# Softmax over rows of 512: the last block's VectorE multiply as seven per-row multiplies

## The chip, the core and the metric

The kernel runs on one core of one Trainium2 chip. The metric is the device time of one execution in microseconds (us), as the median of several executions.

## The reference

The input `x` has 16 x 1024 rows of 512 float32 values. Each row is divided by a temperature of 0.5 and put through a softmax:

```python
x_scaled = x / 0.5
x_max = np.max(x_scaled, axis=-1, keepdims=True)
exp_x = np.exp(x_scaled - x_max)
return (exp_x / np.sum(exp_x, axis=-1, keepdims=True)).astype(np.float32)
```

Every input byte is read once and every output byte is written once: 33.55 MB each way.

## The kernel before

The 16384 rows are cut into 8 chunks (`c` = 0 to 7) of 2048 rows. Each of the 128 partitions holds 16 rows of a chunk, 8192 floats, so a chunk is one SBUF tile `xt` of 4 MB. There are six such tiles; chunks 6 and 7 reuse the tiles of chunks 0 and 1. All work on a chunk is done in place in its tile.

A chunk is worked on in blocks, a block being a range of the 16 rows of a partition: chunk 0 has three blocks (4, 4 and 8 rows), chunks 1 to 6 have one of 16 rows, and chunk 7 has two of 8 rows, which makes 11 blocks (`n` = 11). A block goes through these steps:

- `shift(i)`: VectorE takes the negated row maxima (`negmax`, line 92) and doubles them (`bias`, line 96). If the chunk isn't loaded yet, its load is issued first on SyncE's queue (line 75).
- `exponentials(i, rows)`: ScalarE computes exp(2x + bias) row by row, and adds up each row on the way (`sums`, line 122).
- `scale_vector(i)`: VectorE takes the reciprocals of the sums (`recip`, line 143) and multiplies the first `k` rows of the block with them, all in one `tensor_mul` in which the reciprocals are broadcast along the 512 columns (line 145). `k` is 12 of 16 rows, 7 of 8, or 4 of 4.
- `scale_scalar(i)`: ScalarE multiplies the other rows, one by one, with a per-partition scale (line 156).
- `store(i)`: when the chunk's last block is done, ScalarE's queue issues one store of the whole chunk, 4 MB (line 166).

The order of instructions on each engine is written out by hand (`tc.manual_schedule()`): in each round the exponentials of block i + 1 come first, then the multiplies of block i, the maxima of block i + 2, and the store. Loads of chunks 1 and 3 are issued on ScalarE's queue, and two rows of chunk 7 come in by GpSimd (line 111), started in the middle of chunk 5. SyncE ends the program with a `nop` (line 192) that waits for everything named in the list `finished`, and the end of the program (shown as line 223) waits for what is left, the last store.

The change is in `scale_vector`, for the last block alone (`i == n - 1`): the second half of chunk 7, eight rows, of which VectorE multiplies seven and ScalarE one. Behind it in the program stands only the store of chunk 7.

Of the kernel before, what the change touches and what calls it, by code (L numbers as in the profile page):

```python
# [1 line left out]

# [4 lines left out]


@with_exitstack
def kernel(  # L10
    ctx: ExitStack,
    tc: tile.TileContext,
    x: bass.AP,
    out: bass.AP,
):
    nc = tc.nc
    fp32 = mybir.dt.float32
    P = nc.NUM_PARTITIONS
    AX = mybir.AxisListType.X
    EXP = mybir.ActivationFunctionType.Exp  # L20
    COPY = mybir.ActivationFunctionType.Copy
    MAX = mybir.AluOpType.max

    D = x.shape[-1]
    xf = x.flatten_outer_dims()
    of = out.flatten_outer_dims()
    N = xf.shape[0]

    G = 16
    C = N // (P * G)
    assert C * P * G == N
    xr = xf.rearrange("(c p g) d -> c p g d", p=P, g=G)
    outr = of.rearrange("(c p g) d -> c p g d", p=P, g=G)
    WHOLE = [(0, G)]
    LATE = 2
    LOADS = [[(0, 4), (4, G)]] + [WHOLE] * 6 + [[(0, G - LATE)]]
    BLOCKS = [[(0, 4), (4, 8), (8, G)]] + [WHOLE] * 6 + [[(0, 8), (8, G)]]  # L40
    STORES = [WHOLE] * 8
    BMAX = 16
    BUFS = 6

    data = ctx.enter_context(tc.tile_pool(name="data", bufs=BUFS))
    stats = ctx.enter_context(tc.tile_pool(name="stats", bufs=6))

    ctx.enter_context(tc.manual_schedule())


    warm = stats.tile([P, 1], fp32, name="warm", bufs=1)
    nc.vector.memset(warm, 0.0)  # L52
    nc.scalar.activation(out=warm, in_=warm, func=EXP)  # L53

    chunks = {}
    blocks = [(c, lo, hi) for c in range(C) for lo, hi in BLOCKS[c]]
    n = len(blocks)
    biases, sums, recips = {}, {}, {}

    finished = []  # L60
    data_wait = mybir.DependencyInfo(
        mybir.DependencyClass.Sync, mybir.DependencyReason.DATA
    )
    for c in range(BUFS):
        chunks[c] = data.tile([P, G, D], fp32, name="xt")

    loaded = set()

    def load(c, queue):
        loaded.add(c)  # L70
        if c >= BUFS:
            chunks[c] = chunks[c - BUFS]
        xt = chunks[c]
        for lo, hi in LOADS[c]:
            part = queue.dma_start(out=xt[:, lo:hi, :], in_=xr[c][:, lo:hi, :])  # L75
            if c == 1:
                tc.add_manual_dep(
                    part.ins, finished[0], data_wait, reason="first rows come alone"
                )
            finished.append(part.ins.name)  # L80

    load(0, nc.sync)
    for c in (1, 3):
        load(c, nc.scalar)

    def shift(i):
        c, lo, hi = blocks[i]
        if c not in loaded:
            load(c, nc.sync)
        b = hi - lo  # L90
        negmax = stats.tile([P, BMAX], fp32, name="negmax")
        nc.vector.tensor_reduce(  # L92
            negmax[:, 0:b], chunks[c][:, lo:hi, :], axis=AX, op=MAX, negate=True
        )
        biases[i] = stats.tile([P, BMAX], fp32, name="bias")
        nc.vector.tensor_scalar_mul(biases[i][:, 0:b], negmax[:, 0:b], 2.0)  # L96

    def load_last_rows(signal):
        seen = stats.tile([P, 1], fp32, name="seen", bufs=1)
        copied = nc.gpsimd.tensor_copy(out=seen, in_=signal)  # L105
        finished.append(copied.ins.name)
        c = C - 1
        to = chunks[c - BUFS][:, G - LATE : G, :]
        of_ = xr[c][:, G - LATE : G, :]
        for p0, p1 in ((P - 2, P), (0, P - 2)):  # L110
            part = nc.gpsimd.dma_start(  # L111
                out=to[p0:p1], in_=of_[p0:p1], max_dma_last_dim=4 * D
            )
            finished.append(part.ins.name)

    def exponentials(i, rows):
        c, lo, hi = blocks[i]
        if i not in sums:
            sums[i] = stats.tile([P, BMAX], fp32, name="sums")
        for g in rows:  # L120
            row = chunks[c][:, lo + g, :]
            nc.scalar.activation(  # L122
                out=row,
                in_=row,
                func=EXP,
                bias=biases[i][:, g : g + 1],
                scale=2.0,
                accum_out=sums[i][:, g : g + 1],
            )
            if c == BUFS - 1 and g == 10:  # L130
                load_last_rows(sums[i][:, g : g + 1])


    def scalar_rows(i):
        c, lo, hi = blocks[i]
        return 4 if hi - lo == G else (hi - lo) // 8

    def scale_vector(i):
        c, lo, hi = blocks[i]
        b = hi - lo  # L140
        k = b - scalar_rows(i)
        recips[i] = stats.tile([P, BMAX], fp32, name="recip")
        nc.vector.reciprocal(recips[i][:, 0:b], sums[i][:, 0:b])  # L143
        rows = chunks[c][:, lo : lo + k, :]
        last = nc.vector.tensor_mul(  # L145
            rows, rows, recips[i][:, 0:k].unsqueeze(2).broadcast_to((P, k, D))
        )
        if i == n - 1:
            finished.append(last.ins.name)

    def scale_scalar(i):
        c, lo, hi = blocks[i]
        b = hi - lo
        for g in range(b - scalar_rows(i), b):
            row = chunks[c][:, lo + g, :]
            last = nc.scalar.activation(  # L156
                out=row, in_=row, func=COPY, scale=recips[i][:, g : g + 1]
            )
            if i == n - 1:
                finished.append(last.ins.name)  # L160

    def store(i):
        c, _, end = blocks[i]
        for lo, hi in STORES[c]:
            if hi == end:
                part = nc.scalar.dma_start(
                    out=outr[c][:, lo:hi, :], in_=chunks[c][:, lo:hi, :]
                )
                if c < C - 1:
                    finished.append(part.ins.name)  # L170

    shift(0)
    shift(1)

    def rows(i):
        c, lo, hi = blocks[i]
        cut = 6 if c == 1 else hi - lo
        return range(cut), range(cut, hi - lo)

    exponentials(0, rows(0)[0])  # L180
    for i in range(n):
        if i + 1 < n:
            exponentials(i + 1, rows(i + 1)[0])
        scale_vector(i)
        scale_scalar(i)
        if i + 2 < n:
            shift(i + 2)
        store(i)
        if i + 1 < n:
            exponentials(i + 1, rows(i + 1)[1])  # L190

    seen = nc.sync.nop()
    info = mybir.DependencyInfo(
        mybir.DependencyClass.Sync, mybir.DependencyReason.DATA
    )
    for name in finished:
        tc.add_manual_dep(seen.ins, name, info, reason="leaves one wait for the end")


# [1 line left out]
_INS = ['x']  # L201
_OUTS = [((16, 1024, 512), 'float32')]


# [23 lines left out]
```

## Time and profile before

| What | Value |
|---|---|
| median of 3 runs | 161.92 us (161.68 to 162.12) |
| profiled execution | 161.71 us |
| its span in the profile | 159.9 us |
| VectorE (DVE) busy | 128.3 us, 80% |
| ScalarE (ACT) busy | 109.6 us, 69% |
| GpSimd (POOL) busy | 1.9 us, 1% |
| bytes moved by DMA | 67.13 MB, mean 420 GB/s over the span |

The profile is one execution; its span begins and ends within the 161.71 us of that execution, with 1.8 us outside it. DVE, ACT, POOL and SP are the engines; a name with a q behind it (ACTq) is the engine's queue, which issues DMAs and waits on semaphores. An operation's row gives line, engine, operation, output and input tile, shape in partitions x elements, count, busy time and mean duration.

### The profile page before, as it was taken

How to read it: one execution, taken by the hardware profiler on the slowest of the kernel's cores; microseconds unless marked ns; L12 is line 12 of the kernel's file. 1: busy time of each engine (PE TensorE's matmuls, PEld its weight loads, DVE VectorE, ACT ScalarE, POOL GpSimd, SP SyncE). 2: the span in 40 equal slices, each digit the busy share in tenths (PEclk: the TensorE clock that was granted, in tenths of full speed). 3: DMA queues.
4: the chain of work that ended last, by engine and by line, in shares of the span. 5: the costliest groups of instructions: out<-in, count | busy, mean ns of one | idle time of the engine just before them, and what ended most of it. 6: DMA issues, size and time to landing. Idle time of an engine off the chain costs nothing.

```text
span 159.9 us, 422 instructions
## 1 busy us (share of the span) xinstructions
DVE 128.3 (80%) x45; ACT 109.6 (69%) x285; POOL 1.9 (1%) x7
## 2 busy tenths in 40 slices
DVE  0600599999999999999999999999999999955000
ACT  3070072924899999599959995999699899980000
POOL 0000000000000000000000000040000000000000
DMA  5999999999999999999999989898999999999994
GB/s 189 467 459 459 393 393 508 410 393 467 451 320 461 402 402 508 402 393 484 434 393 443 467 380 492 370 483 384 415 454 436 416 516 393 393 475 443 393 443 205
DMA packets 2642, 67.13 MB, mean 420 GB/s; under 512 B 336, under 2 KB 336, under 8 KB 464
## 3 DMA queue, kind: packets, MB, share of 16 engines
q10 hardware_dynamic: 1440, 41.94, 60.8%
q1 hardware_dynamic: 1008, 24.64, 36.5%
q0 software_dynamic: 192, 0.52, 0.8%
q14 instruction: 2, 0.02, 0.0%
HBM read 33.55 MB, written 33.55 MB: 420 GB/s over the span
## 4 chain that ended last, share of the span: by engine, by line
DVE 66%; ACT 10%; DMA 10%; issue 4%; SPq 0%
DVE negmax L92 39%; DVE xt L145 25%; ACT xt L122 10%; DMA xt<-in_x_dram 10%; DVE recip L143 1%; DVE bias L96 1%; SPq L75 0%
## 5 line engine op out<-in xcount | busy, mean ns | idle before, releaser
L122 ACT ACTIVATE xt<-xt,bias 128x512 f32<-128x512 f32 x128 | 90.4, 708 | 32.9 <-DVE bias L96 31.6
L92 DVE TENSOR_REDUCE negmax<-xt 128x16 f32<-128x8192 f32 (+2 forms) x11 | 69.9, 6353 | 14.2 <-DMA xt<-in_x_dram 14.2
L145 DVE TENSOR_TENSOR xt<-xt,recip 128x6144 f32<-128x6144 f32 (+2 forms) x11 | 55.6, 5056 | 0.4
L122 ACT ACTIVATION_READ_ACCUMULATOR xt<-xt,bias 128x1 f32 x128 | 23.9, 187 | 0.0
L156 ACT ACTIVATE xt<-xt,recip 128x512 f32<-128x512 f32 x27 | 17.3, 706 | 0.0
L143 DVE RECIPROCAL recip<-sums 128x16 f32<-128x16 f32 (+2 forms) x11 | 2.4, 220 | 2.1 <-ACT xt L122 2.1
L96 DVE TENSOR_SCALAR bias<-negmax 128x16 f32<-128x16 f32 (+2 forms) x11 | 1.9, 173 | 0.4
L53 ACT ACT_TABLE_LOAD x1 | 1.3, 1283 | 0.7 <-PEq L212 0.7
L111 POOL DMA_DIRECT2D xt<-in_x_dram x2 | 1.5, 744 | 0.5 <-issue 0.5
L105 POOL COPY seen<-sums 128x1 f32<-128x1 f32 x1 | 0.2, 186 | 105.2 <-ACT xt L122 105.2
L52 DVE MEMSET warm<- 128x1 f32 x1 | 0.1, 59 | 0.8 <-PEq L212 0.8
L53 ACT ACTIVATE warm<-warm 128x1 f32<-128x1 f32 x1 | 0.2, 203 | 0.0
L212 POOL MEMSET const-bfloat16-1.0<- 128x1 bf16 x1 | 0.1, 96 | 0.0
L212 POOL MEMSET const-uint8-127<- 128x1 uint8 x1 | 0.1, 96 | 0.0
L212 POOL MEMSET const-float32-0.0<- 128x1 f32 x1 | 0.1, 93 | 0.2 <-issue 0.2
L212 POOL MEMSET const-float32-1.0<- 128x1 f32 x1 | 0.1, 93 | 0.0
## 6 DMA issues: line engine op xcount, KB each, us to landing
out_dram<-xt ACTq DMA_DIRECT2D x8, 4096.0 KB, 20.9
xt<-in_x_dram SPq DMA_DIRECT2D x4, 4096.0 KB, 45.3
xt<-in_x_dram ACTq DMA_DIRECT2D x2, 4096.0 KB, 31.4
xt<-in_x_dram SPq DMA_DIRECT2D x1, 3584.0 KB, 25.3
xt<-in_x_dram SPq DMA_DIRECT2D x1, 3072.0 KB, 16.4
xt<-in_x_dram SPq DMA_DIRECT2D x1, 1024.0 KB, 4.7
xt<-in_x_dram POOLq DMA_DIRECT2D x1, 504.0 KB, 19.2
xt<-in_x_dram POOLq DMA_DIRECT2D x1, 8.0 KB, 8.6
```

The costliest lines, as they stand in the source:

```text
L52: nc.vector.memset(warm, 0.0)
L53: nc.scalar.activation(out=warm, in_=warm, func=EXP)
L92: nc.vector.tensor_reduce(negmax[:, 0:b], chunks[c][:, lo:hi, :], axis=AX, op=MAX, negate=True)
L96: nc.vector.tensor_scalar_mul(biases[i][:, 0:b], negmax[:, 0:b], 2.0)
L105: copied = nc.gpsimd.tensor_copy(out=seen, in_=signal)
L111: part = nc.gpsimd.dma_start(out=to[p0:p1], in_=of_[p0:p1], max_dma_last_dim=4 * D)
L122: nc.scalar.activation(out=row, in_=row, func=EXP, bias=biases[i][:, g : g + 1], scale=2.0, accum_out=sums[i][:, g : g + 1],)
L143: nc.vector.reciprocal(recips[i][:, 0:b], sums[i][:, 0:b])
L145: last = nc.vector.tensor_mul(rows, rows, recips[i][:, 0:k].unsqueeze(2).broadcast_to((P, k, D)))
L156: last = nc.scalar.activation(out=row, in_=row, func=COPY, scale=recips[i][:, g : g + 1])
L212: nc = _bacc.Bacc("TRN2", target_bir_lowering=False, num_devices=1)
```

## The change

In the last block VectorE no longer multiplies seven rows by one `tensor_mul` with a broadcast operand, but each row of 512 columns by a `tensor_scalar_mul` whose scalar is one reciprocal per partition. The other ten blocks keep the one `tensor_mul`. The end of the program waits for the last of the seven.

```diff
@@ -141,12 +141,16 @@
         k = b - scalar_rows(i)
         recips[i] = stats.tile([P, BMAX], fp32, name="recip")
         nc.vector.reciprocal(recips[i][:, 0:b], sums[i][:, 0:b])
+        if i == n - 1:
+            for g in range(k):
+                row = chunks[c][:, lo + g, :]
+                last = nc.vector.tensor_scalar_mul(row, row, recips[i][:, g : g + 1])
+            finished.append(last.ins.name)
+            return
         rows = chunks[c][:, lo : lo + k, :]
-        last = nc.vector.tensor_mul(
+        nc.vector.tensor_mul(
             rows, rows, recips[i][:, 0:k].unsqueeze(2).broadcast_to((P, k, D))
         )
-        if i == n - 1:
-            finished.append(last.ins.name)
```

## Prediction

> **What bounds the kernel now.** I read the page first, its DMA lines before anything else, because a kernel that reads and writes every byte once can be held by its transfers whatever its engines do.
>
> ```profile
> DMA  5999999999999999999999989898999999999994
> ...
> HBM read 33.55 MB, written 33.55 MB: 420 GB/s over the span
> ```
>
> The DMA engines are busy in every slice between the first and the last, those in which VectorE and ScalarE have nothing left to do included. Next I read the chain of work that ended last, and the timeline of the end.
>
> ```profile
> 142.00 0.02 issue
> 142.02 0.21 DVE recip L143
> 142.24 0.02 issue
> 142.26 3.89 DVE xt L145
> ```
>
> ```profile
> 141.89 1.32 ACT L156 ACTIVATE xt<-xt,recip 128x512 f32<-128x512 f32 x2
> 142.02 0.20 DVE L143 RECIPROCAL recip<-sums 128x8 f32<-128x8 f32 x1 [1.89 <-ACT xt L122]
> 142.26 3.89 DVE L145 TENSOR_TENSOR xt<-xt,recip 128x3584 f32<-128x3584 f32 x1
> 146.24 0.34 ACTq L166 DMA_DIRECT2D out_dram<-xt  x1
> ```
>
> The chain stops with the instruction of the change: the last multiply runs from 142.26 to 146.15, and the last store is issued at 146.24, 0.09 us later. Taken alone this says that a shorter multiply ends the kernel earlier. But 13.7 us of span follow, which the chain doesn't explain. SyncE's waits say what they are, and the DMA issues of the last two stores, asked one by one (the store of chunk 6, issued at 135.85 in the timeline, then that of chunk 7), say how long each took from issue to landing:
>
> ```profile
> SPq L223 <- DMA out_dram<-xt: 9.5, 1, 9.5
> ```
>
> ```profile
> out_dram<-xt ACTq DMA_DIRECT2D x1, 4096.0 KB, 13.6
> ```
>
> ```profile
> out_dram<-xt ACTq DMA_DIRECT2D x1, 4096.0 KB, 12.8
> ```
>
> So chunk 6 lands at 135.85 + 13.6 = 149.45, 3.2 us after the last store was issued, and chunk 7 at 146.24 + 12.8 = 159.04, and then the span is over but for 0.9 us. The landings are 9.6 us apart though the issues were 10.4 apart. What a store needs by itself is its bytes over the rate, so I read the windows (length, busy time of DVE, ACT and POOL, then the clock, the share of the 16 DMA engines, and GB/s):
>
> ```profile
> 142.30:146.20 3.90, 3.85 (x1) 0.91 (x2) 0.00 (x0) 1.00 1.03 445
> 146.60:156.30 9.70, 0.00 (x0) 0.00 (x0) 0.00 (x0) 1.00 1.00 432
> ...
> 146.60:147.80 1.20, 0.00 (x0) 0.00 (x0) 0.00 (x0) 1.00 1.01 437
> 147.80:149.00 1.20, 0.00 (x0) 0.00 (x0) 0.00 (x0) 1.00 1.02 437
> 149.00:150.20 1.20, 0.00 (x0) 0.00 (x0) 0.00 (x0) 1.00 1.01 437
> ```
>
> 4.194 MB at 432 GB/s take 9.7 us. That is the distance between the two landings. The engines were fully busy while the last multiply ran (1.03) and across the change from one store to the next (1.01, 1.02, 1.01; shares slightly over 1 come from counting a packet where it starts). The last store spends its first three microseconds standing behind the store before it. What bounds the end is DMA throughput and not the multiply, in spite of the chain.
>
> **The change part by part.** Durations are from the groups with shapes kept apart:
>
> ```profile
> L145 DVE TENSOR_TENSOR xt<-xt,recip 128x6144 f32<-128x6144 f32 x6 | 39.4, 6558 | 0.2
> L145 DVE TENSOR_TENSOR xt<-xt,recip 128x3584 f32<-128x3584 f32 x3 | 11.7, 3892 | 0.1
> ...
> L96 DVE TENSOR_SCALAR bias<-negmax 128x16 f32<-128x16 f32 x6 | 1.0, 175 | 0.2
> ...
> L96 DVE TENSOR_SCALAR bias<-negmax 128x4 f32<-128x4 f32 x2 | 0.3, 171 | 0.1
> ```
>
> *Removed:* one TENSOR_TENSOR of 3584 elements, 3.89 us, on the path to the issue of the last store.
>
> *Added:* seven TENSOR_SCALAR of 512 elements with one gap of 0.02 us (the chain's "issue" pieces) between each two. The trace has no TENSOR_SCALAR of that length and none with a per-partition scalar, so I bound it. Slow end, if it streams like the multiply: (6558 - 3892) / (6144 - 3584) = 1.04 ns an element and 3892 - 3584 x 1.04 = 160 ns fixed, so 693 ns a row and 7 x 0.693 + 6 x 0.02 = 4.97 us. Slower still, at ScalarE's price for the same row (706 ns, the 27 rows of L156) with a semaphore wait of 0.02 before each as well: 7 x 0.706 + 7 x 0.02 + 6 x 0.02 = 5.20 us. Fast end: the 171 ns of the four-element row, as if length cost nothing, 7 x 0.171 + 0.12 = 1.32 us. The TENSOR_SCALAR rows lie nearest in kind: twelve more elements cost 4 ns, 0.33 ns each, a third of the multiply's slope; that is thin, since it rests on 4 ns. I take 0.45, between them and nearer the row of the same operation: 171 + 508 x 0.45 = 400 ns, so 7 x 0.400 + 0.12 = 2.92 us. VectorE is done about 1.0 us sooner and the last store is issued at about 145.3, with 1.3 us later (147.5) and 2.6 us earlier (143.7) as the ends. ScalarE's own row ends by 143.21, so below that its row would be what is late.
>
> [...]
>
> *On the path or beside it:* neither matters for the end, unless the store comes too late for its turn. With the previous store's packets still running when it is issued, an earlier issue only stands longer in the queue: worth 0. For a later issue the slack is this. The windows show packets starting in rounds of 16, one every 1.21 us, so eight rounds make a store (9.7 / 1.21); in windows of 0.2 us the last store's eighth round starts between 157.0 and 157.4, so its first began 7 x 1.21 us before, near 148.6. From issue to first packet the trace shows one uncovered case, the first load: issued at 0.74, and the DMA share starts in the window 1.70 to 1.80, 1.0 us. So an issue as late as 147.5 to 147.6 still finds its turn, 1.3 us of cover. One engine of the 16 runs a round ahead (the share is 0.95 in the last round, 156.3 to 157.5); it would run dry earlier, but it also finishes a round before the others, so its idle time is free. The slowest bound, 5.20 us, is 1.31 us longer than now and just fits.
>
> *Moved:* nothing. No queue order changes; the store remains the only thing behind the waiting instruction on ACTq, and no maxima, load or exponential follows on VectorE. POOL's work ended long before. The reciprocals and ScalarE's row 15 are as before. `finished` names the last of seven instead of the one; SyncE passes that wait at 149.5 together with chunk 6's landing, so it costs nothing, and even 1.3 us later it would still be early.
>
> *The sum:* span 159.9 + 0 us, plus 1.8 outside it, is the profiled 161.7; that execution lies 0.2 us under the median of the runs. I forecast the median, 161.9.
>
> **The rivals.** *The seven rows cost more than the cover (slower).* Place: the issue of the last store. It decides from 3.89 + 1.3 = 5.2 us for the seven, 725 ns a row with its gap taken off; each microsecond beyond is a microsecond of the end. A row at what ScalarE needs for an exponential with its read-out of the sum (708 + 187 = 895 ns) would make 6.39 us, 2.5 later, less 1.3: about 163.1. To be seen as slower it needs over 5.7 us, 800 ns a row. For it: the trace doesn't show this operation. Against: every VectorE slope here is at most 1.04 ns an element with 160 to 175 ns fixed, for elementwise work. 8%.
>
> *The landing follows the issue (faster).* If the 12.8 us were a latency of the store and not a place in a queue, the end would come as much sooner as the multiply: 161.9 - 1.0 = 160.9, at the fast end of the bounds (2.6 us sooner) 159.3. For it: the chain ends in the multiply. Against: the 9.6 us between landings, and no idle share at the boundary. 10%.
>
> *The change doesn't do what it says.* The rows might run no faster than the old multiply, 4.97 us. Then the issue is at 147.3, still inside the cover: 161.9. This belongs to no change.
>
> **How the numbers follow.** About 0.3%, 0.49 us, is what a measurement of this kernel can tell from no change; the three runs lie 0.44 us apart. No change gets 0.82, faster 0.10, slower 0.08. The range: no change at 161.9 with half a microsecond for the scatter of medians, 161.4 to 162.4. All bounds of the unknown cost, from 1.32 to 5.20 us, give the same end, so they don't widen it, and both other cases, 18% together, stay outside.
>
> **What would show it.** Right: seven TENSOR_SCALAR of 128x512 in place of the last TENSOR_TENSOR, at about 0.4 us; the last store issued near 145.3; its time from issue to landing longer by what the issue is earlier (13.8 us in place of 12.8); the landing near 159.0 and the span at 159.9; the DMA share 1.0 across 148.6. The step on the row's price is wrong if the rows take 0.69 us; the end shouldn't notice. The forecast is wrong if issue to landing stays at 12.8 while the issue moves, or if a window between 147 and 149 shows DMA engines idle.

## The result and the profile after

The changed kernel takes 162.29 us (median of 22 runs) where the kernel before takes 162.04 (22 runs): ratio 1.0016, 95% interval 1.0009 to 1.0024. It is slower by a quarter of a microsecond. That is inside the predicted range and less than the 0.3% that I had called measurable, but it is a difference, and I had forecast none. The profiled execution took 162.25 us with a span of 160.3; 1.95 us lie outside the span, where the kernel before had 1.8.

The step that the change is about went nearly as forecast. First the timeline of the changed kernel at the end, and the group of the new operation:

```profile
142.05 0.20 DVE L143 RECIPROCAL recip<-sums 128x8 f32<-128x8 f32 x1 [1.89 <-ACT xt L122]
142.29 2.86 DVE L147 TENSOR_SCALAR xt<-xt,recip 128x512 f32<-128x512 f32 x7
145.24 0.34 ACTq L170 DMA_DIRECT2D out_dram<-xt  x1
```

```profile
L147 DVE TENSOR_SCALAR xt<-xt,recip 128x512 f32<-128x512 f32 x7 | 2.9, 480 | 0.0
```

Seven rows take 2.86 us where one multiply took 3.89, and the last store is issued at 145.24. A single row reads 480 ns, but 7 x 480 = 3.36 us is more than the 2.86 us they occupy: neighbouring rows overlap, and one row costs 0.41 us of the engine's time. Next the two last stores, asked one by one (chunk 6's, issued at 135.88, then chunk 7's), SyncE's wait for the last, and the windows across the boundary between the stores:

```profile
out_dram<-xt ACTq DMA_DIRECT2D x1, 4096.0 KB, 13.9
```

```profile
out_dram<-xt ACTq DMA_DIRECT2D x1, 4096.0 KB, 14.2
```

```profile
SPq L227 <- DMA out_dram<-xt: 9.5, 1, 9.5
```

```profile
146.60:147.80 1.20, 0.00 (x0) 0.00 (x0) 0.00 (x0) 1.00 1.01 437
147.80:149.00 1.20, 0.00 (x0) 0.00 (x0) 0.00 (x0) 1.00 1.02 437
149.00:150.20 1.20, 0.00 (x0) 0.00 (x0) 0.00 (x0) 1.00 1.01 437
```

The store goes out 1.0 us sooner and takes 1.4 us longer (14.2 against 12.8). The landings, 149.8 and 159.4, are again 9.6 us apart, SyncE again waits 9.5 us, and the DMA engines are as full as before. The microsecond that VectorE gained became waiting time in the DMA queue. Inside the span nothing came of it, and the 0.4 us by which this one span is longer is scatter: the spans of the kernel before, in the executions timed beside the experiments below, average 160.32, 160.27, 160.22 and 160.32 us over 35, 29, 35 and 29 executions, those of the changed kernel 160.30, 160.13 and 160.31 over 22, 12 and 12.

What stays is the time outside the span. Taken as time less span of each execution and averaged, it is 1.78, 1.77, 1.78 and 1.78 us in those runs of the kernel before, and 2.00, 1.97 and 2.00 in those of the changed kernel. One execution scatters by 0.03 us in the kernel before, which is no more than spans given to 0.1 us make by rounding, and by 0.10 to 0.12 in the changed kernel. The difference is 0.2 us, nearly all of the 0.25. In the profile only the DMA queue that it names "instruction" (q14) shows anything behind the span; a packet on it, 8 KB here (82 GB/s over the 0.1 us of the last window below), is called an instruction fetch below, after that name. Its line for the window from 155 to 165 us, kernel before and changed kernel (packets, MB, share of 16 engines):

```profile
q14 instruction: 1, 0.01, 0.3%
```

```profile
q14 instruction: 2, 0.02, 0.5%
```

The changed kernel has one packet more there, and the window 162.1 to 162.2 alone holds it, 1.8 to 1.9 us behind the end of the span (160.3):

```profile
q14 instruction: 1, 0.01, 20.2%
```

### The profile page after: what moved, and what is told of

The parts are those of the page before. It is cut to its first block, busy times and chain, and to the rows that moved or that the text cites. A ratio compares the mean times of both kernels' runs of the same rounds, so it can differ in the third digit from the quotient of the medians.

```text
span 160.3 us, 428 instructions
## 1 busy us (share of the span) xinstructions
DVE 127.3 (79%) x51; ACT 109.5 (68%) x285; POOL 1.9 (1%) x7
## 4 chain that ended last, share of the span: by engine, by line
DVE 65%; DMA 10%; ACT 10%; issue 4%; DVEq 0%; SPq 0%
DVE negmax L92 39%; DVE xt L151 23%; DMA xt<-in_x_dram 10%; ACT xt L122 10%; DVE xt L147 2%; DVE recip L143 1%; DVE bias L96 1%; DVEq L227 0%; SPq L75 0%
## 5 line engine op out<-in xcount | busy, mean ns | idle before, releaser
L92 DVE TENSOR_REDUCE negmax<-xt 128x16 f32<-128x8192 f32 (+2 forms) x11 | 69.9, 6352 | 14.2 <-DMA xt<-in_x_dram 14.2
L151 DVE TENSOR_TENSOR xt<-xt,recip 128x6144 f32<-128x6144 f32 (+2 forms) x10 | 51.7, 5171 | 0.3
L147 DVE TENSOR_SCALAR xt<-xt,recip 128x512 f32<-128x512 f32 x7 | 2.9, 480 | 0.0
```

Of the source, the lines that this page charges most:

```text
L92: nc.vector.tensor_reduce(negmax[:, 0:b], chunks[c][:, lo:hi, :], axis=AX, op=MAX, negate=True)
L147: last = nc.vector.tensor_scalar_mul(row, row, recips[i][:, g : g + 1])
L151: nc.vector.tensor_mul(rows, rows, recips[i][:, 0:k].unsqueeze(2).broadcast_to((P, k, D)))
```

## The experiments

**Is there a difference, and does it come with the issue of the store or with the instructions?** Two of these runs are the two kernels again, unchanged.

> The kernel before once more, unchanged, timed as if it were a new kernel. It measures what two equal programs can differ by. All theories expect a ratio of 1.000 with an interval that holds 1. If the 0.16% of the change is of the size that two loads of the same program differ by (theory 'scatter'), this ratio may lie as far from 1 as 0.1 to 0.2%.

Measured: 161.94 us (12 runs), ratio 0.9998 (0.9987 to 1.0008); 1.78 us outside the span. Equal programs are equal, to 0.1%.

> The changed kernel once more, beside the others on the same chip. If the loss belongs to the change, the ratio is again 1.0016, within about 0.001 (some 0.25 us). Theory 'scatter': the ratio is nearer to 1.000.

Measured: 162.07 us, ratio 0.9997 (0.9981 to 1.0012). The time alone doesn't repeat the loss here, since its spans average 160.13; twelve executions of a span that scatters by some tenths can't show 0.2 us. The time outside the span can: 1.97. The profiled execution of this run is one that doesn't have the loss (161.72 us with a span of 159.9, 1.8 outside), and in it the window 155 to 165 has a single instruction packet. So the extra packet and the loss were absent together in this one execution.

> The kernel before, but its last multiply covers four of the seven rows (three rows of each partition in the last block stay unscaled). As many instructions as before, of the same kinds; only the last store is issued earlier, by 3 x 512 x 1.04 ns = 1.6 us, at about 144.6. Theory 'issue' (an earlier issue of the last store lengthens the end): slower, by 0.2 to 0.4 us. Theory 'program' (six more VectorE instructions shift what the DMA engines do besides the stores, long before the end): the same as before, 1.000 within 0.001. Theory 'latency' (the landing follows the issue, the rival of the prediction): 1.6 us faster, ratio 0.990.

```diff
+        if i == n - 1:
+            k = 4
         rows = chunks[c][:, lo : lo + k, :]
```

Measured: ratio 0.9999 (0.9984 to 1.0013), 1.77 us outside the span. The timeline and the time from issue to landing:

```profile
142.31 2.29 DVE L147 TENSOR_TENSOR xt<-xt,recip 128x2048 f32<-128x2048 f32 x1
144.69 0.34 ACTq L168 DMA_DIRECT2D out_dram<-xt  x1
```

```profile
out_dram<-xt ACTq DMA_DIRECT2D x1, 4096.0 KB, 14.5
```

Issued 1.55 us sooner than before, the store takes 1.7 us longer. An earlier issue neither helps nor harms. 'Latency', which asked for 1.6 us less, falls by the ratio. 'Issue' asked for 0.2 to 0.4 us more, and the interval of the ratio only just reaches 0.2; it falls by the time outside the span, where the loss lies and where nothing is added here.

> The kernel before with its single last multiply, and six memsets of one element per partition ahead of the last reciprocal, where VectorE waits 1.89 us for ScalarE; so VectorE has as many instructions as in the changed kernel, and the last store is issued when it is now, at 146.2. Theory 'program': slower by as much as the change, ratio 1.0016. Theory 'issue': the same as before, 1.000 within 0.001.

```diff
+        if i == n - 1:
+            pad = stats.tile([P, 1], fp32, name="pad", bufs=1)
+            for _ in range(6):
+                nc.vector.memset(pad, 0.0)
         recips[i] = stats.tile([P, BMAX], fp32, name="recip")
```

Measured: 162.18 us, ratio 1.0007 (0.9991 to 1.0022), which again can't decide; 2.02 us outside the span, with the scatter of the changed kernel (0.13), and two instruction packets behind the span. The old multiply, with six instructions more that do nothing, has the changed kernel's loss.

**By the instruction, or by a limit?**

> The kernel before with one memset of one element per partition ahead of the last reciprocal, in VectorE's idle time: one VectorE instruction more, where the change has six more. Looked at is the time less the span of the same execution: 1.78 us in the kernel before, 2.0 us in the changed kernel. Theory 'tail, a step' (VectorE's instruction stream has grown over a limit beyond which more of it is fetched behind the span): either 1.78 or 2.0 and nothing between, depending on where the limit lies. Theory 'tail, by the instruction' (each costs 0.035 us): 1.82 us. Theory 'scatter' (nothing but chance): no information.

Measured: ratio 1.0017 (1.0003 to 1.0030); 2.04 us outside the span on average, 2.00 to 2.10 in all twelve executions (scatter 0.03), where the kernel before beside it has 1.77. A single instruction costs 0.27 us.

> The kernel before with 24 such memsets ahead of the last reciprocal: 24 VectorE instructions more. Their time (24 x about 0.06 us = 1.4 us, after the 1.89 us in which VectorE is idle) shouldn't delay the last store by more than a few tenths, which the cover takes. Theory 'tail, a step': the time less the span is 2.0 us, as in the changed kernel. Theory 'tail, by the instruction': 1.78 + 24 x 0.035 = 2.6 us. The span is 160.2 as in the kernel before in either case.

Measured: ratio 1.0006 (0.9997 to 1.0015); 1.78 us outside the span. Twenty-four cost nothing there, so it isn't by the instruction; but my 'step' forecast 2.0 and is wrong too. The instruction packet had moved into the span: this is the window 140.0 to 140.2, where the kernel before has none between 139.5 and 141.

```profile
q14 instruction: 1, 0.01, 9.7%
```

The same run delays the last store, since the memsets outlast the idle time (23 of them take 2.81 us, where I had expected 1.4 for all): issued at 147.09, 0.85 us later than before, it still found its turn (the share is 1.02 from 147.8 to 149.0).

> The changed kernel, in which six of the eleven blocks (chunks 1 to 6) use the negated maximum itself as the bias of the exponential and not its double, so that six VectorE instructions go elsewhere; the softmax is the same function with any shift. VectorE has as many instructions as in the kernel before, and the last store is issued at about 145.2 as in the changed kernel. Theory 'tail' (the number of VectorE instructions): the time less the span is back at 1.78 us, and the time at that of the kernel before, ratio 1.000. Theory 'per-row multiply' (the new operation itself costs the 0.2 us): 2.0 us as in the changed kernel.

```diff
+        if 3 <= i < 9:
+            biases[i] = negmax
+            return
         biases[i] = stats.tile([P, BMAX], fp32, name="bias")
```

Measured: 161.82 us, ratio 0.9994 (0.9983 to 1.0005); 1.77 us outside the span. With the seven rows kept and VectorE's count back at the old number the loss is gone. The per-row multiply itself costs nothing outside the span. Against the kernel before this version is the same. The six doublings lay on VectorE's path, so the last store went out at 144.02, earlier than the 145.2 that I had expected; this too neither helped nor harmed. The counts are what they are meant to be: over the whole trace, semaphore instructions and drains included, VectorE has 53 records in the kernel before, 59 in the changed kernel and 53 here.

> The kernel before, whose last multiply runs over the last twelve rows that VectorE and ScalarE share (rows 3 to 14 of the chunk, all by the first row's reciprocals, so that these rows are scaled wrongly): 6.56 us in place of 3.89, with no instruction more, and the last store issued 2.67 us later, at 148.9. Theory 'cover' (the prediction's: the previous store covers 1.3 us): 2.67 - 1.3 = 1.4 us slower, ratio 1.008 to 1.009, and DMA engines idle between 147.5 and 150. Theory 'latency' (the landing follows the issue): 2.7 us slower, ratio 1.0165. The time less the span stays at 1.78 us.

```diff
         rows = chunks[c][:, lo : lo + k, :]
-        last = nc.vector.tensor_mul(
-            rows, rows, recips[i][:, 0:k].unsqueeze(2).broadcast_to((P, k, D))
-        )
+        by = recips[i][:, 0:k].unsqueeze(2).broadcast_to((P, k, D))
+        if i == n - 1:
+            rows = chunks[c][:, lo + k - 12 : lo + k, :]
+            by = recips[i][:, 0:1].unsqueeze(2).broadcast_to((P, 12, D))
+        last = nc.vector.tensor_mul(rows, rows, by)
```

Measured: 163.35 us (4 runs), ratio 1.0079 (1.0066 to 1.0093). Timeline, time from issue to landing, and the windows across the boundary:

```profile
142.75 6.56 DVE L149 TENSOR_TENSOR xt<-xt,recip 128x6144 f32<-128x6144 f32 x1 [0.41 <-ACT xt L158]
149.40 0.34 ACTq L168 DMA_DIRECT2D out_dram<-xt  x1
```

```profile
out_dram<-xt ACTq DMA_DIRECT2D x1, 4096.0 KB, 11.1
```

```profile
147.80:149.00 1.20, 1.20 (x1) 0.00 (x0) 0.00 (x0) 1.00 0.07 27
149.00:150.20 1.20, 0.31 (x1) 0.00 (x0) 0.00 (x0) 1.00 0.00 0
150.20:151.40 1.20, 0.00 (x0) 0.00 (x0) 0.00 (x0) 1.00 1.01 437
```

Here the cover is gone. A share counts a packet where it starts, so the two low windows don't mean 2.4 us of idle engines: the last full packets of chunk 6's store start by 148.0 (the window 148 to 150 holds 15 packets, each under 512 bytes) and take 1.21 us each (16 of them make the share of 1.01 in 1.20 us), and the next full ones start at about 150.2, which leaves the DMA engines idle for about 1.4 us by my estimate, a little over one round. The multiply had to wait for ScalarE's row, which I had overlooked, so the issue came 3.16 us later and not 2.67. The span averages 161.3, 1.0 us more than before's 160.3; by the two profiles it is 1.4 more, as much as the idle time. So 1.75 us were covered by the two profiles, 2.15 by the averages, more than my 1.3. A part of that is the start of the store: 0.8 us from its issue (149.40) to its first full packets, where I had taken 1.0 from the first load. 'Latency' would have asked for 3.2. The remainder is outside the span, 2.05 us and not the 1.78 that I expected, and the profile offers a reason: the new wait is a VectorE instruction too (54 records in the whole trace, against 53). The semaphore instructions on VectorE's queue at the multiply's line, kernel before and this one:

```profile
L145 DVEq EVENT_SEMAPHORE  x1: 21/21/21, 135.9 to 135.9; - x1
```

```profile
L149 DVEq EVENT_SEMAPHORE  x2: 21/21/21, 136.1 to 142.4; - x2
```

One instruction more, and the time outside the span is that of the one memset.

**Does the fetch move, and does the loss end where it leaves the tail?**

> The changed kernel a third time, beside the version below that has 18 instructions more. Theory 'fetch in the tail' (six more VectorE instructions carry the end of VectorE's stream over a limit, and the fetch of what lies beyond it falls behind the span): the time less the span is again about 2.0 us, the ratio to before 1.001 to 1.002.

Measured: 162.32 us, ratio 1.0018 (1.0002 to 1.0034); 2.00 us outside the span; two instruction packets behind it, the second in the window from 162.2.

> The changed kernel with 18 memsets of one element per partition ahead of the last reciprocal: 24 VectorE instructions more than in the kernel before, 18 more than in the changed one. Theory 'fetch in the tail': as in the version with 24 memsets the limit is reached inside the span, where the fetch is hidden; the time less the span is 1.78 us, and the kernel with more instructions is 0.2 us faster than the changed one, ratio to before 1.000. Theory 'by the instruction': slower than the changed kernel, 2.0 us or more less the span.

Measured: 162.22 us, ratio 1.0012 (0.9997 to 1.0026); 1.77 us outside the span, scatter 0.03, with an instruction packet in the window 140.2 to 140.4. Eighteen further instructions removed the loss outside the span, as expected; the time wasn't 0.2 us better than the changed kernel's, as I had also expected, because its spans average 160.47 (changed kernel 160.31). Whether that 0.16 us is scatter or the price of a fetch among the last stores is open.

> The kernel before with twelve memsets ahead of the last reciprocal, between the six that cost 0.2 us and the 24 that cost nothing. Theory 'fetch in the tail': between the two, with executions of 1.78 and of about 2.05 us less the span, or all of them 1.78 if the limit is already reached inside the span. Theory 'by the instruction': 1.78 + 0.4 = 2.2 us.

Measured: ratio 1.0029 (1.0012 to 1.0046), from spans that average 160.66 where the kernel before beside them has 160.22. That is more than the whole loss of the change, and I have no reason for it; it stays open. Outside the span there are 1.77 us. An instruction packet starts between 160.6 and 160.8, right behind the span's end at 160.4:

```profile
q14 instruction: 1, 0.01, 11.7%
```

> The kernel before with six memsets on GpSimd in place of VectorE (behind its loads, long before the end). Theory 'fetch in the tail' with a limit for each engine's own stream: 1.78 us less the span as in the kernel before, unless GpSimd's stream happens to end at such a limit too. Theory 'program' (the size of the program as a whole): 2.0 us as in the changed kernel.

Measured: ratio 1.0005 (0.9992 to 1.0018); 1.78 us outside the span, one instruction packet behind it. The program's size as a whole isn't it.

> The kernel before with three memsets in VectorE's idle time. Theory 'fetch in the tail': between one more (2.04 us less the span in every execution) and six more (1.8 to 2.2 us), so 2.04 to 2.1 us in all or nearly all executions; an instruction fetch, if the record reaches that far, more than 1.87 us behind the end of the span, where it lay with six more. Theory 'chance of the program's placement': any value, 1.78 as likely as 2.0.

Measured: 162.45 us, ratio 1.0026 (1.0011 to 1.0041); 2.19 us outside the span on average, 2.15 to 2.24 in all executions (scatter 0.03), more than I expected. No second packet stands in the record, which may end too soon: the latest that any of these traces holds lies 1.87 us behind its span.

> The kernel before with nine memsets in VectorE's idle time. Theory 'fetch in the tail': between six more (fetch 1.87 us behind the end of the span, cost 0.2 us) and twelve more (fetch 0.33 us behind it, no cost), so the fetch lies between 0.33 and 1.87 us behind it, and the time less the span is 1.78 us or between that and 2.0. Theory 'chance of the program's placement': any value.

Measured: ratio 1.0011 (0.9994 to 1.0027); 1.82 us outside the span. The second instruction packet lies in the window 161.5 to 161.6, with the span's end at 160.3:

```profile
q14 instruction: 1, 0.01, 22.6%
```

> The kernel before with six activations of one element per partition on ScalarE ahead of its last multiply (6 x about 0.2 us, on an engine that is done 2.9 us before VectorE there). Theory 'fetch in the tail' with a limit for each engine's own stream: ScalarE's stream is elsewhere against its own limits, so 1.78 us less the span is likeliest; 2.0 would say that its end lies near a limit too. The span is as in the kernel before.

```diff
+        if i == n - 1:
+            for _ in range(6):
+                nc.scalar.activation(out=warm, in_=warm, func=COPY)
         recips[i] = stats.tile([P, BMAX], fp32, name="recip")
```

Measured: ratio 1.0006 (0.9990 to 1.0022); 1.78 us outside the span. A different packet moved: the one that every other kernel here has 1.0 to 1.3 us behind the span is gone from there, and the window 148.5 to 148.7 has one instead.

```profile
q14 instruction: 1, 0.01, 9.7%
```

Six ScalarE instructions moved it, so I take it for ScalarE's; behind the span it had cost nothing, since the time outside is 1.78 us with it and without.

Put together, by VectorE instructions more than before:

| more | outside the span, us | the fetch that moves |
|---|---|---|
| 0 (before, again, short multiply, changed less six) | 1.77 to 1.78 | none |
| 1 (one memset; the longer multiply's wait) | 2.04, 2.05 | none in the record |
| 3 | 2.19 | none in the record |
| 6 (changed kernel three times, memsets) | 1.97 to 2.02, single executions 1.74 to 2.19 | 1.9 us behind the span (absent in one execution, and the loss with it) |
| 9 | 1.82 | 1.2 us behind |
| 12 | 1.77 | 0.3 us behind |
| 24 (memsets; changed kernel with 18) | 1.77 to 1.78 | inside, 20 us before the end |

## Why the prediction was right and wrong

**The row's price: right.** 2.86 us for seven rows against my 2.92, and the issue at 145.24 against about 145.3. Part of this is luck. A single row is recorded at 480 ns, 80 above the 400 that I took from the thin slope of the short TENSOR_SCALAR rows, and neighbours overlap by about 80 ns ((3.36 - 2.86) / 6) where I had put a gap of 20; the two errors nearly cancel.

**On the path or beside it: right.** An earlier issue is worth nothing (1.0 and 1.55 us sooner, spans unchanged), a later one is covered (0.85 us later with 24 memsets, share still 1.02), and beyond the cover the DMA engines fall idle (3.16 us later, share 0.07 and 0.00). The 1.3 us of cover was too small; 1.75 to 2.15 were seen. The last store did not stand three microseconds behind the one before it, as I wrote at first, but 2.4, from 146.24 to the 148.6 of my own later working.

**The chain: rightly not believed.** It ended in the multiply of the change, and shortening the multiply by 1.0 us changed no landing.

**The sum: wrong.** The step that failed is "span 159.9 + 0 us, plus 1.8 outside it". I took the 1.8 us as a constant of the program. It is 1.78 with VectorE's old instruction count and 2.00 with six more, and this is what the change did to the time. Under "Added" I counted the six further instructions by their execution alone, which is hidden; the packets of the queue "instruction", which lay 1.9, 1.2 and 0.3 us behind the span with six, nine and twelve VectorE instructions more, stood in no step. The 0.3% that I called the least a measurement can tell rested on three executions; 22 of each kernel told 0.16% from nothing, with an interval of 0.08% either way. Of the rivals, the slower one had the right sign with the wrong place: the place was not the issue of the store.

**What is shown, and what is argued.** Shown: the loss lies outside the span, comes with VectorE's count and with no other part of the change, isn't proportional to it, and is gone when an instruction fetch that moves with the count lies earlier (0.3 us behind the span or inside it). Argued: that VectorE waits for this fetch in what it does behind the kernel. No VectorE record lies behind the span, and with one and three more the fetch itself isn't in the record, so that another source of their loss isn't excluded. Why three cost more than one is open too. What VectorE does behind the span no run shows. Measured are packets of 8 KB and, with one, three and six instructions more, 0.2 to 0.4 us more outside the span.

## What to carry to other kernels

Before costing a step at the end of the chain, ask what the last transfer is waiting for: where landings are one transfer time apart (here 9.6 us, with 9.7 for a store's bytes at the rate of its windows) and the DMA share stays at 1.0 across the boundary, an earlier issue only waited longer in the queue (1.4 us longer for 1.0 sooner, 1.7 for 1.55). Where a difference of 0.1 to 0.3% matters, look at the time less the span beside the span; in the kernel before it scattered by 0.03 us where the span scattered by 0.2 to 0.3, and it found the place of the loss that the medians could not. An instruction that was free on its engine still cost 0.2 to 0.4 us behind the kernel here, and a few more or fewer took that away again; that it is a fetch of instructions that costs is the likeliest reading, not a shown one.

## What the runs showed of the hardware that was not expected

One VectorE instruction more, of 59 ns in idle time, lengthened the time outside the span by 0.27 us, three by 0.41, nine by 0.04 and twelve by nothing. Seven TENSOR_SCALAR of 512 float32 elements with a per-partition scalar took 2.86 us, 0.41 us each, though each is recorded as 480 ns.
